# Gate and up as seven block products in place of eight, on equal token halves

## The chip, the core and the metric

The kernel runs on one core of a Trainium2 chip. Its engines work beside each other, each in its own fixed order of instructions, and wait for one another through semaphores: PE multiplies matrices (a matmul here is a 128x128 block of weights times up to 512 columns of activations) and writes to PSUM; DVE and POOL do elementwise work; ACT does elementwise work with a scale, a bias or a function; SP issues most transfers. The metric is the device time of one execution in microseconds, the median of several runs.

## The reference

Two transformer-like layers run over 128 prompt tokens and 512 sample tokens that share all weights. The model width is 1024, the width of the feed-forward part 2816. A layer has a mixer (short convolution, windowed attention and a gated delta rule, side by side), and then the part that this change is in:

```python
h2 = _rms(x, p['norm2_g']) * (1 + sc2) + sh2
x = x + g2 * ((jax.nn.silu(h2 @ p['w_gate']) * (h2 @ p['w_up'])) @ p['w_down'])
```

The vectors sc2, sh2 and g2 come from a conditioning vector of each token group (adaLN), so the prompt's 128 tokens have others than the sample's 512. Everything is float32.

## The kernel before

All activations of the feed-forward part are feature-major: a tile holds 128 features in its partitions and tokens in its columns, all 640 of them (the prompt first). The operands of a product are in the form fp32r, and each is split in a high part (a rounded copy, made by ACT) and a low part (the exact rest, made by DVE, or by POOL for some tiles of the norm). A product of two such operands takes three matmuls: high by high, low by high, high by low (`split` L173 and L174, `fm_product` L200 to L206). The tokens are taken in two parts, HB, of 256 and 384.

The feed-forward stage of a layer runs so:

- The mixer's output product (`rows` with w_out) adds to the residual `xt`, feature tile by feature tile (`residual`, L446); its last four feature tiles are one late group (LATE_OUT): first part 0 of all four, then the normalisation of part 0 (`Norm.half`), then part 1 and its normalisation. The normalisation squares, sums over the features on PE (L379, L381), takes the root on POOL (L386), spreads it over the partitions on PE (L389, into the bank `pkq`), and then makes per feature tile a scaled value t on DVE (L418), the high part on ACT (L423, L424, L427) and the low part on DVE or POOL (L425, L431).
- Gate and up: feature tiles f = 0 to 21 of 128 columns of w_gate and w_up. Per tile, 8 k tiles x 3 passes x 2 parts, 48 matmuls for gate and as many for up. Then tanh on ACT (L1524), silu on DVE (L1526), the product with up (L1533) and the split of the result. In the first two tiles (LEAD) the low parts of the activations come last, and part 0 of both tiles before part 1.
- Down: the 22 tiles are done in three chunks (FF_CHUNKS: 8, 8 and 6). After each chunk its rows of w_down are multiplied with it, one output feature tile at a time, and added to xt. In the last chunk of layer 0 the last three output tiles (LATE_DOWN) form a late group, with the next layer's norm behind each part; in layer 1 each finished tile is transposed, copied (L1560) and stored.
- Weights come as 512 KB transfers on SP's queue, three raw buffers deep; ACT and DVE split each (`load_w`, 128x1024 a tile). Between them stand steps of the next layer's adaLN product (`drain(gen, 1)`).

The order on each engine is set by a scheduler that follows the program order with priorities; what stands in it is seen below.

Of the kernel before, what the change touches and what calls it, by code (L numbers as in the profile page):

```python
# [23 lines left out]
KT_ = 8  # L24
TOK = 640
NT = 5
HB = ((0, 256), (256, 640))      # the two parts of the tokens that one product takes
HN = (256, 384)
# [12 lines left out]
FF_CHUNKS = ((0, 8), (8, 8), (16, 6))  # L41
WK_BUFS, CV_BUFS = 4, 4
RAW_BUFS, W_BUFS, SIDE_BUFS = 3, 2, 2
SG_BUFS, LEAD = 4, 2
# [8 lines left out]
LATE_DOWN = (5, 6, 7)  # L53

# column layout of the packed constants
# [8 lines left out]
def shape_constants():  # L64
    """Constants that depend on the shapes alone, packed as [128, C_TOTAL] float32."""
# [33 lines left out]
    near = 16 * (p // 64)              # first row of the near half of a 32-block: the half solved first  # L99
# [9 lines left out]
def hybrid_trunk_kernel(  # L109
# [15 lines left out]
    def atiles(pool, tag, name):  # L125
        """(hi, lo) of both token parts of one feature tile."""
        return tuple(tuple(pool.tile([128, HN[h]], F32R, tag=f"{tag}{h}", name=f"{name}{h}{x}", bufs=16) for x in "hl")
                     for h in range(2))

    def spans(a0, a1):  # L130
        """tokens a0..a1 cut at the parts' border: (part, columns of the part, tokens from a0)."""
        return [(h, slice(max(a0, b0) - b0, min(a1, b1) - b0), slice(max(a0, b0) - a0, min(a1, b1) - a0))
                for h, (b0, b1) in enumerate(HB) if max(a0, b0) < min(a1, b1)]

# [20 lines left out]
    # ---------------------------------------------------------------- constants  # L155
# [72 lines left out]
    # ---------------------------------------------------------------- small per-layer vectors  # L228
    # silu of the conditioning vectors: columns (sample, prompt) per k-tile, padded to 32
# [63 lines left out]
    def ada_pair(l, f, araw):  # L293
        """half f of the columns of the 1024-column pieces 0 and 1; a generator as ada."""
# [41 lines left out]
    class Norm:  # L336
# [10 lines left out]
        def ft(self, n, name):  # L347
            return self.fp.tile([128, n], F32, tag="ft", name=name, bufs=6)
# [1248 lines left out]
```

## Time and profile before

| | |
|---|---|
| median of 3 runs | 1807.85 us (1805.13 to 1810.63) |
| span of the profiled execution | 1806.5 us |
| median less that span | 1.35 us |
| PE busy in the span | 1725.5 us (96%) |
| DVE busy | 981.2 us (54%) |
| ACT busy | 636.2 us (35%) |
| POOL busy | 113.2 us (6%) |

The span is the time from the first to the last instruction of one execution that was recorded by the hardware profiler. The runs are timed without it, and what lies around a span isn't in the page; the difference above stands for it. The page's busy time of PE counts a matmul from its start to the modelled end, and neighbouring matmuls overlap, so a matmul's worth is the distance between two starts, not its duration. "Idle before" in a row is the time in which that engine waited just before the row's instructions, with the instruction that ended it.

### The profile page before, as it was taken

The numbers are of one execution on the slowest core, as the hardware profiler recorded it, in microseconds if no ns is written. First come the engines' busy times: TensorE is split into PE (matmuls) and PEld (weight loads), VectorE is DVE, ScalarE is ACT, GpSimd is POOL, SyncE is SP. The second block draws the span as 40 slices with busy tenths as digits, with TensorE's granted clock in tenths as the row PEclk, the third lists the DMA queues.
The fourth block names the chain that finished last, engine by engine and source line by source line (L and its number), as shares of the span: only waits on it lengthen the run. The fifth ranks groups of instructions, "written<-read, shape, count | busy, mean of one in ns | idle before, by whom it ended". The sixth has DMA issues, their size and how long they took to land. (4 is left out here: it accounts for less than half of the span.)

```text
span 1806.5 us, 34244 instructions
## 1 busy us (share of the span) xinstructions
PE 1725.5 (96%) x14179; PEld 1566.9 (87%) x14179; DVE 981.2 (54%) x2324; ACT 636.2 (35%) x1330; POOL 113.2 (6%) x230
## 2 busy tenths in 40 slices
PE   5998999999999999999999879999999999999998
PEld 3887875488999999999988879655899999999998
DVE  3799767666433333333477995777563333333333
ACT  3545244544322122212255442556352212221221
POOL 1111112000000000000012011220010000000000
PEclk7999999999999999999999989999999999999999
DMA  8512234656242222222232222455722222222222
GB/s 287 174 48 68 80 105 126 204 165 227 70 134 78 82 71 80 73 72 78 91 106 72 60 60 77 144 150 161 231 59 71 71 82 70 82 71 73 80 66 75
DMA packets 230025, 188.41 MB, mean 104 GB/s; under 512 B 11566, under 2 KB 206062, under 8 KB 229870
## 3 DMA queue, kind: packets, MB, share of 16 engines
q1 hardware_dynamic: 212992, 170.70, 31.4%
q10 hardware_dynamic: 16878, 15.53, 2.7%
q8 instruction: 111, 1.82, 0.4%
q14 instruction: 44, 0.36, 0.1%
HBM read 168.64 MB, written 17.56 MB: 103 GB/s over the span
## 5 line engine op out<-in xcount | busy, mean ns | idle before, releaser
L173 ACT CAST whi<-raw 128x1024 fp32r<-128x1024 f32 (+2 forms) x191 | 190.2, 996 | 598.9 <-PE pmm L202 271.5
L174 DVE TENSOR_TENSOR wlo<-raw,whi 128x1024 fp32r<-128x1024 f32 (+2 forms) x191 | 220.9, 1158 | 224.3 <-ACT whi L173 223.1
L200 PE MATMUL pmm<-hhi,whi 128*128 128x256 f32 x1008 | 319.0, 317 | 6.6 <-ACT dnp L517 5.3
L203 PE MATMUL pmm<-hhi,wlo 128*128 128x256 f32 x1008 | 317.4, 316 | 7.1 <-DVE wlo L174 7.1
L202 PE MATMUL pmm<-hlo,whi 128*128 128x256 f32 x960 | 301.7, 314 | 0.0
L200 PE MATMUL pmx<-hhi,whi 128*128 128x384 f32 (+1 forms) x688 | 213.0, 310 | 1.0 <-ACT hhi L427 0.7
L203 PE MATMUL pmx<-hhi,wlo 128*128 128x384 f32 (+1 forms) x688 | 212.9, 310 | 0.0
L200 PEld LDWEIGHTS pmm<-hhi,whi 128*128 128x128 f32 x1008 | 195.9, 194 | 11.1 <-ACT dnp L517 6.1
L203 PEld LDWEIGHTS pmm<-hhi,wlo 128*128 128x128 f32 x1008 | 195.7, 194 | 8.4 <-DVE wlo L174 7.7
L202 PE MATMUL pmx<-hlo,whi 128*128 128x256 f32 (+1 forms) x640 | 197.6, 309 | 0.0
L202 PEld LDWEIGHTS pmm<-hlo,whi 128*128 128x128 f32 x960 | 185.7, 193 | 0.7 <-issue 0.4
L200 PEld LDWEIGHTS pmx<-hhi,whi 128*128 128x128 f32 x688 | 130.3, 189 | 2.5 <-ACT hhi L427 1.5
L203 PEld LDWEIGHTS pmx<-hhi,wlo 128*128 128x128 f32 x688 | 130.3, 189 | 0.4 <-issue 0.4
L202 PEld LDWEIGHTS pmx<-hlo,whi 128*128 128x128 f32 x640 | 121.3, 190 | 0.0
L1533 DVE SCALAR_TENSOR_TENSOR av<-sg,pmx 128x256 f32<-128x256 f32 (+1 forms) x88 | 42.9, 488 | 131.8 <-PE pmx L203 123.9
L446 DVE SCALAR_TENSOR_TENSOR xt<-pmx,mod,xt 128x128 f32<-128x128 f32 (+1 forms) x96 | 39.1, 436 | 96.2 <-PE pmx L203 96.0
L446 DVE SCALAR_TENSOR_TENSOR xt<-pmm,mod,xt 128x128 f32<-128x128 f32 (+1 forms) x96 | 39.0, 436 | 91.6 <-PE pmm L203 89.1
L492 PE MATMUL pmm<-wlo,hhi 128*128 128x256 f32 x240 | 69.2, 289 | 0.7 <-DVE wlo L174 0.7
L491 PE MATMUL pmm<-whi,hhi 128*128 128x256 f32 x240 | 69.7, 292 | 0.0
L493 PE MATMUL pmm<-whi,hlo 128*128 128x256 f32 x240 | 69.3, 289 | 0.0
L1524 ACT ACTIVATE th<-pmm 128x256 f32<-128x256 f32 (+1 forms) x88 | 38.2, 434 | 76.7 <-PE pmm L203 70.7
L1526 DVE SCALAR_TENSOR_TENSOR sg<-th,pmm 128x256 f32<-128x256 f32 (+1 forms) x88 | 42.6, 485 | 41.1 <-ACT th L1524 41.1
(450 smaller groups left out, 3798.0 us busy)
## 6 DMA issues: line engine op xcount, KB each, us to landing
adaw<-in_ada_w_dram SPq DMA_DIRECT2D x64, 512.0 KB, 3.9
raw<-in_w_gate_dram SPq DMA_DIRECT2D x44, 512.0 KB, 3.9
raw<-in_w_up_dram SPq DMA_DIRECT2D x44, 512.0 KB, 3.9
raw<-in_w_in_dram SPq DMA_DIRECT2D x36, 512.0 KB, 4.8
araw<-in_ada_w_dram SPq DMA_DIRECT2D x32, 512.0 KB, 5.0
raw<-in_w_down_dram SPq DMA_DIRECT2D x32, 512.0 KB, 4.1
raw<-in_w_down_dram SPq DMA_DIRECT2D x16, 384.0 KB, 3.6
xm<-xscr SPq DMA_DIRECT2D x16, 320.0 KB, 4.9
```

The costliest lines, as they stand in the source:

```text
L173: (hi_eng or A.copy)(hi, src)
L174: (lo_eng or V).tensor_tensor(out=lo, in0=src, in1=hi.bitcast(F32), op=ALU.subtract)
L200: mm(o, lhsT=wh[:, k], rhs=ah, start=k == 0, stop=False)
L202: mm(o, lhsT=wh[:, k], rhs=al, start=False, stop=False)
L203: mm(o, lhsT=wl[:, k], rhs=ah, start=False, stop=not lead and k == n - 1)
L446: V.scalar_tensor_tensor(out=x[:, sl], in0=pt[:, a0:a1], scalar=gate[:, g:g + 1], in1=x[:, sl], op0=ALU.mult, op1=ALU.add)
L491: mm(pt, lhsT=ah[:, ts], rhs=wh[:, k % 4], start=k == 0, stop=False)
L492: mm(pt, lhsT=ah[:, ts], rhs=wl[:, k % 4], start=False, stop=False)
L493: mm(pt, lhsT=al[:, ts], rhs=wh[:, k % 4], start=False, stop=k == 7)
L1524: A.activation(th, pg[:, 0:n], AF.Tanh, scale=0.5)
L1526: V.scalar_tensor_tensor(out=sgs[h], in0=th, scalar=1.0, in1=pg[:, 0:n], op0=ALU.add, op1=ALU.mult)
L1533: V.scalar_tensor_tensor(out=av, in0=sgs[h], scalar=0.5, in1=pu[:, 0:n], op0=ALU.mult, op1=ALU.mult)
```

## The change

Two feature tiles of gate (or of up) are computed together as a 2 x 2 block product: the weights in blocks of 2 halves of k (four k tiles each) by 2 feature tiles, the activations in blocks of 2 halves of k by 2 halves of the tokens. Eight block products become seven, in the form of Strassen and Winograd: some operands are sums of blocks, and some results are sums of products. Token parts are now 320 and 320. The core of the diff:

```diff
-HB = ((0, 256), (256, 640))
+HB = ((0, 320), (320, 640))
-FF_CHUNKS = ((0, 8), (8, 8), (16, 6))
+FF_CHUNKS = ((0, 4), (4, 4), (8, 4), (12, 4), (16, 4), (20, 2))
-LATE_DOWN = (5, 6, 7)
+LATE_DOWN = tuple(range(8))
...
+    class PairNorm(Norm):
...
+        def half(self, h):
...
+            for j in range(4):
+                h12, h22 = self.ft(HH, "h12"), self.ft(HH, "h22")
+                self.value(j, 1, h12)
+                self.value(j + 4, 1, h22)
+                h11, h21 = self.first[j][:, 0], self.first[j][:, 1]
+                t3, t1, t2, t4 = (self.ft(HH, name) for name in ("nt3", "tt1", "tt2", "nt4"))
+                G.tensor_tensor(out=t3, in0=h12, in1=h22, op=ALU.subtract)
+                G.tensor_tensor(out=t1, in0=h12, in1=h11, op=ALU.subtract)
+                G.tensor_tensor(out=t2, in0=h22, in1=t1, op=ALU.subtract)
+                G.tensor_tensor(out=t4, in0=h21, in1=t2, op=ALU.subtract)
+                for name, src in (("nt3", t3), ("t1", t1), ("t2", t2), ("nt4", t4)):
+                    self.block(j, name, src, self.fp if n < 12 else apool)
...
+            held = pkq()
+            Y, Z = held[:, 0, 0:HH], held[:, 1, 0:HH]
+            for bank in (Y, Z):
+                mm(bank, lhsT=identr, rhs=B[0]["b11"][0], start=True, stop=True)
...
+                    with tc.high_priority():
+                        split(flat(D), flat(self.d[0]), flat(self.d[1]))
+                        V.tensor_tensor(out=flat(Pa), in0=flat(D), in1=flat(O)[:, 1:2].to_broadcast([128, 2, 512]), op=ALU.add)
+                        split(flat(Pa), flat(self.a[0]), flat(self.a[1]))
+                        split(O[:, 0], *self.o)
+                        V.tensor_tensor(out=Pb[:, 0], in0=Pa[:, 1], in1=D[:, 0], op=ALU.add)
+                        V.tensor_tensor(out=Pb[:, 1], in0=Pb[:, 0], in1=O[:, 0], op=ALU.add)
+                        split(flat(Pb), flat(self.b[0]), flat(self.b[1]))
+                def product(self, bank, w, name, start):
+                    wh, wl = w
+                    for j in range(4):
+                        bh, bl = B[j][name]
+                        mm(bank, lhsT=wh[:, j], rhs=bh, start=start and j == 0, stop=False, skip_group_check=True)
+                        mm(bank, lhsT=wh[:, j], rhs=bl, start=False, stop=False, skip_group_check=True)
+                        mm(bank, lhsT=wl[:, j], rhs=bh, start=False, stop=j == 3, skip_group_check=True)
...
+                def s4(self, hold=False):
+                    if hold:
+                        A.copy(Y, self.kept)
+                    self.product(Y, self.of(self.b, 0), "t2", False)
+                    A.copy(Z, Y)
+                    self.u = tp("u")
+                    A.copy(self.u, Y)
...
+                if ci == 0:
+                    p, q = Pair(*pairs[0]), Pair(*pairs[1])
+                    for step in (p.s1, p.s3, lambda: q.s1(True), q.s3, p.s2, p.s4, p.s5, p.s6, q.s2, p.s7, lambda: q.s4(True),
+                                 q.s5, q.s6):
+                        step()
...
+                for ms in (LATE_DOWN,) if last_chunk and norm else tuple((m, m + 1) for m in range(0, KT_, 2)):
+                    drain(gen, None if last_chunk else 1)
+                    rows(ms, w_down[l], f0, nf, act, mods[l][:, 40:48], norm if last_chunk else None, True,
+                         nf - 2 if ms == (0, 1) else None)
```

Each `product` is 12 matmuls of 320 columns (L1645 to L1647), and a pair of feature tiles has seven: s1 with the block b11 of the first token half, s3 with b21, and s2, s4, s5, s6, s7 with nt3, t2, nt4, t1 and nb22, all from the second half or from both. D holds two weight blocks, O the other two, and Pa and Pb are their sums (L1634, L1637, L1638, DVE); D, Pa, Pb and one block of O are split. Y and Z are two accumulators in one bank that is held for the whole stage and is the same kind of tile as the one that holds the norm's spread root. s1 copies its result, negated, to Y; s2 copies its own to w7; s4 copies Y to Z and to u; s5 and s6 add u and w7 on DVE (c21, c22). The down product takes its first two output tiles with the chunk's last two feature tiles last (`lead` = nf − 2). Residual adds are now of 128, 192 and 320 columns (L528).

On PE, where layer 0's feed-forward stage starts, before: the sums (L381) and the spread (L389) of part 1 stand among first-part products; hhi and hlo are the norm's high and low parts, whi and wlo those of the weights.

```order
1882 L381 MATMUL pxo<-ones_c,sq 128x1 x3
1883 L206 MATMUL pmx<-hlo,whi 128x256 x4
1884 L389 MATMUL pkq<-ident,ny 128x128 x3
1885 L206 MATMUL pmx<-hlo,whi 128x256
1886 L203 MATMUL pmm<-hhi,wlo 128x256
1887 L200 MATMUL pmm<-hhi,whi 128x256
...
1901 L206 MATMUL pmm<-hlo,whi 128x256 x8
1902 L200 MATMUL pmx<-hhi,xhi 128x256
```

Now, at the same place: b_ are blocks of the first half, nt_ are nt3 of j = 0 to 3, ohi is the high part of O.

```order
1869 L406 MATMUL pkq<-ident,ny 128x80 x4
1870 L1645 MATMUL pmm<-b_5606,whi 128x320
...
1874 L1645 MATMUL pmx<-nt_5747,xhi 128x320
...
1878 L1645 MATMUL pmx<-nt_5778,xhi 128x320
...
1881 L1645 MATMUL pmx<-nt_5809,xhi 128x320
...
1884 L1606 MATMUL pkq<-b_5579,identr 128x320 x2
1885 L1645 MATMUL pmm<-b_5614,ohi 128x320
...
1897 L1645 MATMUL pmx<-nt_5840,xhi 128x320
```

Behind the spread came a long row of products with first-part activations (1885 to 1901 and on); now three matmuls with b_ remain there (1870 to 1872), and the products with nt3 of three j's stand ahead of the two that fill the held bank (L1606) and of p.s3 (ohi).

On ACT, the second token part of that stage, before: each tile's high part is one ACTIVATE or an ACTIVATE and a CAST.

```order
439 L427 ACTIVATE hhi<-t_5759,mod_97 128x384
440 L423 ACTIVATE t_5766<-t_5764,mod_97 128x384
441 L173 CAST act0h<-av 128x256
442 L424 CAST hhi<-t_5766 128x384
443 L427 ACTIVATE hhi<-t_5772,mod_97 128x384
444 L1524 ACTIVATE th<-pmm 128x256
445 L423 ACTIVATE t_5780<-t_5778,mod_97 128x384
446 L424 CAST hhi<-t_5780 128x384
```

And now: L482 is a value of the second half, L469 the high part of a block, L513 that of nb22.

```order
467 L482 ACTIVATE h_5731<-t_5733,mod_97 128x320
468 L482 ACTIVATE h_5732<-t_5736,mod_97 128x320
469 L469 CAST nt_5747<-nt_5739 128x320
470 L469 CAST t_5750<-tt_5740 128x320
471 L469 CAST t_5753<-tt_5741 128x320
472 L469 CAST nt_5756<-nt_5742 128x320
473 L513 ACTIVATE nb_5759<-h_5732 128x320
474 L482 ACTIVATE h_5762<-t_5764,mod_97 128x320
475 L482 ACTIVATE h_5763<-t_5767,mod_97 128x320
476 L469 CAST nt_5778<-nt_5770 128x320
```

Two values, four high parts and nb22 of one j now stand ahead of the next j's values (474, 475).

On POOL at the same place, before: L386 is the root, L425 a low part of the norm.

```order
84 L386 TENSOR_TENSOR ny<-nms,mhalf 128x3
85 L425 TENSOR_TENSOR hlo<-t_5766,hhi 128x384
86 L425 TENSOR_TENSOR hlo<-t_5780,hhi 128x384
87 L425 TENSOR_TENSOR hlo<-t_5794,hhi 128x384
```

Now: four operations per j on values that ACT makes (h_), 16 in the stage.

```order
82 L503 TENSOR_TENSOR nt_5739<-h_5731,h_5732 128x320
83 L504 TENSOR_TENSOR tt_5740<-h_5731,h_5573 128x320
84 L505 TENSOR_TENSOR tt_5741<-h_5732,tt_5740 128x320
85 L506 TENSOR_TENSOR nt_5742<-h_5573,tt_5741 128x320
86 L503 TENSOR_TENSOR nt_5770<-h_5762,h_5763 128x320
```

POOL's low parts went to DVE, and the sums nt3, tt1, tt2 and nt4 came in their place.

## Rows read from the trace of the kernel before

**Rows 1.** Windows: the two FFN stretches and the layer-1 start; busy (count) per engine.
```profile
core 0: us, PE busy (x) PEld busy (x) DVE busy (x) ACT busy (x) POOL busy (x), PEclk, DMA share, GB/s
441.00:936.00 495.00, 492.62 (x3404) 485.06 (x3397) 195.72 (x345) 126.26 (x212) 8.51 (x10) 0.99 0.30 89
1337.00:1802.00 465.00, 462.29 (x3139) 460.51 (x3139) 173.17 (x284) 109.59 (x168) 3.05 (x3) 1.00 0.25 72
1322.70:1337.00 14.30, 13.43 (x101) 12.83 (x100) 9.37 (x25) 6.66 (x17) 1.63 (x2) 0.92 0.22 65
```

**Rows 2.** Timeline of PE: start, duration; steps of 384, 256, 272 columns.
```profile
527.85 0.34 PE L200 MATMUL pmm<-hhi,whi 128*128 128x384 f32 x1
...
532.02 0.28 PE L200 MATMUL pmx<-hhi,whi 128*128 128x256 f32 x1
...
534.89 0.34 PE L200 MATMUL pmx<-hhi,whi 128*128 128x384 f32 x1
...
947.79 0.29 PE L491 MATMUL pmm<-zw,hhi 128*128 128x272 f32 x1
...
951.06 0.29 PE L493 MATMUL pmm<-zw,hlo 128*128 128x272 f32 x1
```

**Rows 3.** Groups by form, DVE: line, names, shapes, count | busy us, mean ns | idle.
```profile
L174 DVE TENSOR_TENSOR wlo<-raw,whi 128x1024 fp32r<-128x1024 f32 x160 | 195.6, 1224 | 213.2 <-ACT whi L173 213.0
...
L174 DVE TENSOR_TENSOR act1l<-av,act1h 128x384 fp32r<-128x384 f32 x44 | 24.3, 552 | 1.2 <-ACT act1h L173 1.2
...
L174 DVE TENSOR_TENSOR act0l<-av,act0h 128x256 fp32r<-128x256 f32 x44 | 19.2, 437 | 19.9 <-ACT act0h L173 19.9
...
L174 DVE TENSOR_TENSOR wlo<-raw,whi 128x512 fp32r<-128x512 f32 x16 | 11.0, 686 | 1.9 <-ACT whi L173 1.7
```

**Rows 4.** Groups by form, ACT, same columns.
```profile
L173 ACT CAST whi<-raw 128x1024 fp32r<-128x1024 f32 x160 | 167.8, 1049 | 528.5 <-PE pmm L202 250.9 <-PE pmx L202 225.1 <-issue 22.5
...
L173 ACT CAST act1h<-av 128x384 fp32r<-128x384 f32 x44 | 22.4, 509 | 6.6 <-DVE av L1533 6.6
...
L173 ACT CAST act0h<-av 128x256 fp32r<-128x256 f32 x44 | 17.9, 406 | 85.9 <-DVE av L1533 85.9
...
L427 ACT ACTIVATE hhi<-t,mod 128x384 fp32r<-128x384 f32 x20 | 12.0, 614 | 16.5 <-DVE t L418 16.5
```

**Rows 5.** Groups by form, POOL: low parts of the norm, same columns.
```profile
L425 POOL TENSOR_TENSOR hlo<-t,hhi 128x384 fp32r<-128x384 f32 x12 | 12.5, 1044 | 22.9 <-ACT hhi L424 22.4 <-PE pmx L206 0.6
...
L425 POOL TENSOR_TENSOR hlo<-t,hhi 128x256 fp32r<-128x256 f32 x12 | 10.5, 874 | 54.2 <-ACT hhi L424 54.2
```

**Rows 6.** Timeline of DVE, layer-1 FFN start: start, duration, what, [idle before <-releaser].
```profile
1311.84 0.61 DVE L446 SCALAR_TENSOR_TENSOR xt<-pmx,mod,xt 128x128 f32<-128x128 f32 x2 [0.80 <-PE pmx L203]
...
1316.76 2.16 DVE L418 SCALAR_TENSOR_TENSOR t<-xt,msc,pkq 128x128 f32<-128x128 f32 x8 [0.21 <-PE pkq L389]
...
1320.75 1.57 DVE L431 SCALAR_TENSOR_TENSOR hlo<-t,mod,hhi 128x128 fp32r<-128x128 f32 x2
...
1322.51 0.60 DVE L431 SCALAR_TENSOR_TENSOR hlo<-t,mod,hhi 128x128 fp32r<-128x128 f32 x2
...
1329.22 0.61 DVE L446 SCALAR_TENSOR_TENSOR xt<-pmx,mod,xt 128x384 f32<-128x384 f32 x1
...
1336.09 2.19 DVE L418 SCALAR_TENSOR_TENSOR t<-xt,msc,pkq 128x384 f32<-128x384 f32 x4 [0.77 <-PE pkq L389]
```

**Rows 7.** Timeline of POOL and ACT in the same stretch.
```profile
1319.95 2.22 POOL L425 TENSOR_TENSOR hlo<-t,hhi 128x256 fp32r<-128x256 f32 x2 [3.99 <-ACT hhi L424]
...
1339.30 1.02 POOL L425 TENSOR_TENSOR hlo<-t,hhi 128x384 fp32r<-128x384 f32 x1 [4.80 <-ACT hhi L424]
...
1338.71 0.52 ACT L424 CAST hhi<-t 128x384 fp32r<-128x384 f32 x1
```

**Rows 8.** Windows at the border of the layers, columns as in rows 1.
```profile
905.00:916.00 11.00, 10.54 (x83) 10.22 (x81) 5.47 (x15) 2.83 (x5) 0.69 (x1) 1.00 0.58 172
916.00:950.00 34.00, 32.15 (x200) 30.06 (x201) 26.48 (x54) 22.77 (x49) 6.75 (x14) 0.95 0.34 97
```

**Rows 9.** Timeline of PE, last transposes of the kernel.
```profile
1801.63 0.55 PE L1556 MATMUL pmx<-ident,xt 128*128 128x128 f32 x3 [0.60 <-DVE xt L446]
```

More of the change, by code (lines that the diff above doesn't have):

```diff
@@ L206, in fm_product, with fm_part @@
                 mm(o, lhsT=wh[:, k], rhs=acts[k][h][1], start=False, stop=k == n - 1)
+    def fm_part(pt, wh, wl, acts, h, ks, first, last):
+        o = pt[:, 0:HH]
+        for k in ks:
+            ah, al = acts[k][h]
+            mm(o, lhsT=wh[:, k], rhs=ah, start=first and k == ks[0], stop=False)
+            mm(o, lhsT=wh[:, k], rhs=al, start=False, stop=False)
+            mm(o, lhsT=wl[:, k], rhs=ah, start=False, stop=last and k == ks[-1])
     def rsqrt_dve(src, n, scale, eps, posts, name):
@@ L344, in __init__ @@
             self.bc = [None, None]
-            self.out = [[None, None] for _ in range(KT_)]
+            self.out = [None] * KT_
         def ft(self, n, name):
-            return self.fp.tile([128, n], F32, tag="ft", name=name, bufs=6)
+            return self.fp.tile([128, n], F32, tag=self.tag, name=name, bufs=self.bufs)
         def add(self, k, parts=(0, 1)):
@@ L410, in high @@
             b0, b1 = HB[h]
[L411 removed]
+            n = HH
             sh, bc_ = self.sh, self.bc[h]
[L413 to L414 removed]
+            if self.out[k] is None:
+                self.out[k] = Act(apool, "a", "h")
+            hi, lo = self.out[k][h]
             x = self.xt[k][:, b0:b1]
@@ L433, in high, with __init__, ft, block @@
             return low
+    class PairNorm(Norm):
+        def __init__(self, fp, xt, a_fn, sh, late):
+            super().__init__(fp, xt, a_fn, sh, late)
+            self.out = [{} for _ in range(4)]
+            self.first = [None] * 4
+        def ft(self, n, name):
+            return self.fp.tile([128, n], F32, tag="tp", name=name, bufs=TP_BUFS)
+        def block(self, j, name, src, pool):
+            if pool is apool:
+                b = pool.tile([128, 2, HH], F32R, tag="a", name=name, bufs=16)
+            else:
+                b = pool.tile([128, 2, HH], F32R, tag="bx", name=name, bufs=12)
+            A.copy(b[:, 0], src)
+            V.tensor_tensor(out=b[:, 1], in0=src, in1=b[:, 0].bitcast(F32), op=ALU.subtract)
+            self.out[j][name] = (b[:, 0], b[:, 1])
+        def value(self, k, h, dst):
+            b0, b1 = HB[h]
+            segs = ((1, slice(0, 128)), (0, slice(128, HH))) if h == 0 else ((0, slice(0, HH)),)
+            t1 = self.ft(HH, "t1")
+            for g, sl in segs:
+                V.scalar_tensor_tensor(out=t1[:, sl], in0=self.xt[k][:, b0:b1][:, sl], scalar=self.a_[0][:, k, g:g + 1],
+                                       in1=self.bc[h][:, sl], op0=ALU.mult, op1=ALU.mult)
+            for g, sl in segs:
+                A.activation(dst[:, sl], t1[:, sl], AF.Identity, bias=self.sh[:, k, g:g + 1])
+        def half(self, h):
+            if 0 not in self.a_:
+                self.a_[0] = self.a_fn(0, KT_)
+            self.stats(h)
+            if h == 0:
+                for i in range(2):
+                    for j in range(4):
+                        if i == 0:
+                            self.first[j] = self.fp.tile([128, 2, HH], F32, tag="act", name="h0", bufs=8)
+                        self.value(j + 4 * i, 0, self.first[j][:, i])
+                        self.block(j, ("b11", "b21")[i], self.first[j][:, i], apool)
+                return
+            n = 0
+            for j in range(4):
[10 more added lines that the diff above has]
+                    self.block(j, name, src, self.fp if n < 12 else apool)
+                    n += 1
+                pool = self.fp if n < 12 else apool
+                n += 1
+                b = pool.tile([128, 2, HH], F32R, tag="a" if pool is apool else "bx", name="nb22", bufs=16 if pool is apool else 12)
+                A.activation(b[:, 0], h22, AF.Copy, scale=-1.0)
+                V.scalar_tensor_tensor(out=b[:, 1], in0=h22, scalar=-1.0, in1=b[:, 0].bitcast(F32), op0=ALU.mult, op1=ALU.subtract)
+                self.out[j]["nb22"] = (b[:, 0], b[:, 1])
```

251 lines of the change are left out of this document (149 added, 102 removed).

## The prediction

> **What bounds the kernel now.** I read the page's busy shares first (PE 96% of the span, DVE 54%, ACT 35%, POOL 6%), then a table of windows, then groups by form, and last the order of time at the start of a feed-forward stage. The two stretches of gate, up and down products, one per layer, hold PE busy 492.62 of 495 us and 462.29 of 465 us at granted clock 0.99 and 1.00, while DVE works 40% of them and ACT 25% [rows 1]. PE is idle 5 us in 960. So a matmul left out there is worth its full spacing, as long as the new work beside PE really stays beside it. That has two places: the steady pairs, where DVE has room, and the start of each feed-forward stage, where the activations are prepared and PE has little else to do.
>
> **What a matmul is worth.** Mean durations of PE rows overlap, so I take starts: 24 matmuls of 384 columns take 532.02 − 527.85 = 4.17 us, 173.8 ns each; 24 of 256 take 2.87 us, 119.6 ns each [rows 2]. A straight line through both gives 146.7 ns at 320 and 126.4 at 272; the trace has 26 steps of 272 in 3.27 us, 125.8 ns [rows 2]. I use 146.4 ns. A pair of feature tiles had 96 matmuls of 320 columns on average and now has 84. There are 44 pairs (11 gate and 11 up in each of two layers), so 44 × 12 × 0.1464 = **−77.3 us**. The down product keeps its columns: 0. Equal halves alone: 0.
>
> **Durations at 320 columns**, between the rows of 256 and 384: a DVE low part or sum 0.49 us (0.437, 0.552) [rows 3]; an ACT cast or copy 0.46 (0.406, 0.509), an ACT scale with bias 0.56 (under 0.614 at 384) [rows 4]; a POOL tensor_tensor 0.96 (0.874, 1.044) [rows 5]; a DVE scaled value t from its spacing, 2.16 us for eight of 128 and 2.19 for four of 384, so 0.27 and 0.55, hence 0.34 at 192 and 0.48 at 320 [rows 6].
>
> **The start of the feed-forward stage.** Before, first-half products need only the high and low parts of the normed activations, and the second part's preparation runs behind them. Now five operand blocks per j (nt3, t1, t2, nt4, nb22) come from both token halves, for j = 0 to 3. In the order of PE the third step of the list, p.s3, stands behind products of nt3 of j = 0, 1 and 2 and behind the two matmuls that fill the held bank, and that bank is the one out of which the last j's values are read. So PE waits for nearly the whole preparation. I count from the start of the last residual add of the first half (in the layer-1 stage 1311.84 [rows 6]).
> First values: +4.9, as before (1316.76). DVE's list up to the last second-half residual: 8 × (0.27 + 0.34) = 4.9 of values, 8 × 0.49 = 3.9 of low parts, two weight low parts 2 × 1.22 and two half sums 2 × 0.69 [rows 3], four residual adds, put at 0.55 as a low part of 384 [rows 3], one square sum 0.49: 15.3. That ends at +20.2. From there to the first second-half value passed 1336.09 − 1329.83 = 6.3 us before [rows 6] (squares, their sums on PE, the root, the spread), and the same steps stand now: +26.5. Two values, two biases and hops: first h22 at +28.2.
> Then one cycle per j, serial as ACT and DVE have it in their order: the next j's values stand on DVE behind this j's nb22 low part, that behind ACT's nb22, that behind ACT's cast of nt4, and that waits for the fourth POOL operation. 4 × 0.96 + 0.46 + 0.46 + 0.49 + 2 × 0.48 + 0.56 + five hops of 0.07 (an ACT cast that ends at 1339.23 lets POOL start at 1339.30 [rows 7]) = 7.1 us. Three cycles bring the last h22 to +49.5; POOL 3.84, then on ACT nt4, nb22, the cast of O (512 columns, between 0.51 and 1.05 [rows 4], 0.62), tanh and hops, before q.s3 can start: about +55.5 to 56.
> PE's work until then: 48 second-half output products (7.0 us), 58 matmuls of the new order (8.5) and sums, spreads and adaLN steps (near 3): 18.5. Idle 37.3, of which 0.9 was there before (13.43 busy of 14.30 in 1322.7 to 1337 [rows 1]): +36.4 a layer. If DVE and ACT overlap neighbouring instructions better than the means, 30; with collisions of DVE and POOL, 44.
> On these: two low parts took 1.57 us beside two POOL operations and 0.60 with POOL idle [rows 6, 7], and the new list sets three low parts per j beside POOL. I let 0.15 us a cycle of it onto the path and take 37 a layer, **+74 us** (60 to 88).
> [...]
>
> **Steady pairs.** PE now needs 84 × 0.1464 = 12.3 us a pair. DVE: four weight operations of 1024 columns (4 × 1.22: low parts of D, Pa, Pb and the sum Pa), three of 512 (3 × 0.69) [rows 3], 7.0 us; and in a gate pair six of 320 columns (four sg, c21, c22; 2.9), in an up pair ten (4.9): 9.9 and 11.9, mean 10.9, 88% of PE's time. Before, DVE had 40% of these stretches. ACT has some 7.4 us. So the weight work hides, but the short waits between copies (Y, Z, u, w7) and the products that follow them do not always: 0 to 0.4 us a pair, I take 0.2 × 40 = **+8** (0 to 16). Ramp after the start, with weight buffers late: **+3** (0 to 6). Six down chunks in place of three: products of the first four tiles of a group cover the last up product's chain (0.49 + 0.46 + 0.49), but in each layer's last chunk, of two tiles, nothing leads: 2 × 1.5 = **+3** (0 to 6).
>
> **Between the layers.** Before, PE is idle 0.46 + 1.85 us in 905 to 950 [rows 8]: three tiles stand in the late group, and their second part's products (54 matmuls of 384, 9.4 us) cover the first part's normalisation. Now all eight stand in it, with two k each: 48 matmuls, 7.0 us, and four of their residual adds stand on DVE behind the normalisation of the first half, a list of 15 us. At least the cover lost, 2.4 us, at most the list uncovered, 14: **+8**.
> **The end.** After the last product came one tile's transposes, copy and store; PE waited 0.60 us for the residual there [rows 9]. Now two tiles come at once and eight tiles leave inside 14 us of PE: **+4** (0 to 8).
> **The clock.** The granted clock is 0.92 in 1322.7 to 1337 [rows 1], where PE waits 0.9 us, so the stage's start has a dip now. The long wait will have one too; what runs slowly inside the wait costs nothing, and what comes behind it may. 0 ± 3.
>
> **Sum:** −77.3 + 74 + 8 + 3 + 3 + 8 + 4 = +22.7. The profiled span is 1806.5 us, 1.35 under the median of the runs (1807.85); I add the same 1.35: 1806.5 + 22.7 + 1.35 = **1830.5 us**.
>
> **Rivals.**
> *B, the preparation is mostly hidden.* If POOL runs its 16 operations nearly back to back (three cycles of 3.84 in place of 7.1) and the first half's list is shorter by its overlaps, idle falls to 20 a layer; with 12 for all the rest −77.3 + 40 + 12 = −25: 1782.5, faster. For it: back-to-back DVE values take 0.27, not their mean. Against: the fixed order of ACT and DVE, which puts j + 1 behind j. It decides below 25 us a layer.
> *C, DVE becomes the bound of gate and up.* Its 88% is an average; an up pair has 11.9 of 12.3. Waits on ACT and collisions of 1.4 us a pair close the mean gap; at 2.4 PE waits a full 1.0 us a pair: 40 × 1.0 in place of 8, 1862, slower.
> *D, the change doesn't gain what it says:* a matmul of 320 columns spaced as one of 384 (173.8 ns): 27 ns × some 6000 matmuls, over 1950. The 272 rows speak against it.
>
> **Chances.** Forecast 0.62 (own range 1808 to 1852), B 0.18, C 0.17, D 0.03. A measurement here tells about 0.3% (5.4 us) from no change. Faster: B's 0.18 less its part near zero, 0.03, plus 0.02 of the forecast's low tail, 0.17; same: that 0.03 and 0.05 of the forecast, 0.08; slower 0.75. The range 1794 to 1862 leaves out most of B (0.12) and D with half of C's tail (0.08).
>
> **What would show it.** Right: after the first b11 products PE idles some 37 us a layer, its waits naming the casts and low parts of nt3, t1 and O; 16 POOL rows of about 0.96 us per layer, every four of them 7 us after the last four; PE's spacing 146 ns at 320 columns; pairs 12.3 to 12.7 us apart. Wrong: a j cycle near 4 us (B), pairs over 13 us with PE waiting on low parts of weights (C), PE idle under 5 us between the layers.

## The result and the profile after

The changed kernel takes 1881.63 us (median of 4 runs, 1875.28 to 1885.66) against 1806.62 for the kernel before on the same chip: a ratio of 1.0401, 95% interval 1.0371 to 1.0431, 75 us slower. 1830.5 was forecast, in a range of 1794 to 1862. The sign was right, the size three times too small.

The page's busy line of the kernel after (it was 96%, 54%, 35% and 6%):

```profile
PE 1710.1 (91%) x13741; PEld 1519.0 (81%) x13741; DVE 1262.7 (67%) x2796; ACT 799.2 (43%) x1644; POOL 131.0 (7%) x250
```

Windows of the kernel after: the two stretches of gate, up and down, and four of 10 us at the start of layer 0's; columns as in [rows 1] (PEld is PE's loading of weights).

```profile
448.70:941.00 492.30, 455.20 (x3004) 429.79 (x3004) 309.47 (x516) 192.26 (x331) 15.66 (x17) 0.96 0.29 85
1373.60:1862.00 488.40, 447.63 (x2899) 431.02 (x2898) 310.62 (x519) 192.53 (x331) 15.65 (x17) 0.95 0.22 65
450.00:460.00 10.00, 3.49 (x16) 1.35 (x15) 7.70 (x17) 5.78 (x17) 0.00 (x0) 0.80 0.52 157
460.00:470.00 10.00, 9.67 (x52) 8.91 (x51) 0.92 (x3) 0.18 (x1) 1.01 (x1) 0.50 0.00 0
470.00:480.00 10.00, 4.46 (x20) 1.60 (x19) 5.13 (x10) 4.98 (x11) 5.78 (x7) 0.50 0.33 105
480.00:490.00 10.00, 2.32 (x5) 1.17 (x5) 7.08 (x12) 4.51 (x10) 5.20 (x6) 0.50 0.00 0
```

PE is idle 37 and 41 us in the two stretches, where it was 2 or 3 [rows 1], and at the start the granted clock is 0.50 for some 30 us. DVE's busy share went from 40% to 63%.

PE in the same stretch of the kernel after, timeline:

```profile
458.62 1.06 PE L286 MATMUL pdn<-adaw,c 128*32 128x256 f32 x2 [6.51 <-DMA adaw<-in_ada_w_dram]
...
479.20 0.64 PE L1645 MATMUL pmx<-nt,xhi 128*128 128x320 f32 x1 [3.12 <-ACT nt L469]
...
486.02 0.64 PE L1645 MATMUL pmx<-nt,xhi 128*128 128x320 f32 x1 [5.24 <-ACT nt L469]
...
490.92 0.87 PE L1606 MATMUL pkq<-b,identr 128*128 128x320 f32 x2 [3.32 <-DVE t L479]
...
502.01 0.31 PE L1645 MATMUL pkq<-t,xhi 128*128 128x320 f32 x1
...
503.62 0.31 PE L1647 MATMUL pkq<-t,xlo 128*128 128x320 f32 x1
...
966.84 0.61 PE L199 MATMUL pmm<-hh,whi 128*128 128x320 f32 x1 [8.09 <-DVE xt L528]
```

Rows 502.01 and 503.62 are 11 steps of 320 columns in 1.61 us, 146.4 ns: the gain per matmul is the one forecast from [rows 2]. Ahead of them PE waits for the cast of nt3 once per j, and for the last value t before it may fill the held bank, as forecast. The row at 966.84 is the border of the layers: 8.09 us for a residual add.

POOL and then DVE beside it, timelines (DVE's rows: last residual add of the first half and of the second, [rows 6] for before; the mean squares; the first second-half values; a low part beside POOL and one after it):

```profile
477.80 0.86 POOL L503 TENSOR_TENSOR nt<-h,h 128x320 f32<-128x320 f32 x1 [3.07 <-ACT h L482]
...
480.62 0.99 POOL L506 TENSOR_TENSOR nt<-h,tt 128x320 f32<-128x320 f32 x1
...
484.62 0.86 POOL L503 TENSOR_TENSOR nt<-h,h 128x320 f32<-128x320 f32 x1 [3.01 <-ACT h L482]
```

```profile
435.92 0.68 DVE L528 SCALAR_TENSOR_TENSOR xt<-pmx,mod,xt 128x128 f32<-128x128 f32 x2 [0.73 <-PE pmx L202]
...
457.20 0.55 DVE L528 SCALAR_TENSOR_TENSOR xt<-pmx,mod,xt 128x320 f32<-128x320 f32 x1
...
465.91 0.16 DVE L401 TENSOR_SCALAR nms<-pxo 80x4 f32<-80x4 f32 x1 [8.17 <-PE pxo L398]
...
469.24 1.01 DVE L479 SCALAR_TENSOR_TENSOR t<-xt,msc,pkq 128x320 f32<-128x320 f32 x2 [3.17 <-PE pkq L406]
...
480.00 0.90 DVE L470 TENSOR_TENSOR t<-tt,t 128x320 fp32r<-128x320 f32 x1 [0.17 <-ACT t L469]
...
482.14 0.49 DVE L470 TENSOR_TENSOR nt<-nt,nt 128x320 fp32r<-128x320 f32 x1 [0.17 <-ACT nt L469]
```

A j cycle is 484.62 − 477.80 = 6.82 us (7.1 forecast), a sum on POOL 0.86 to 0.99 (0.96 forecast). A low part takes 0.49 us alone and 0.90 beside POOL; [rows 6, 7] had that in two rows.

A border between two chunks of layer 1, DVE and then PE: the new pairs' weight work (pa, pb and their low parts xlo) and a low part of the down product's own weights (wlo<-raw) stand between the parts of residual adds, and PE waits for these.

```profile
1556.43 0.34 DVE L528 SCALAR_TENSOR_TENSOR xt<-pmm,mod,xt 128x128 f32<-128x128 f32 x1
1556.69 1.22 DVE L173 TENSOR_TENSOR xlo<-pa,xhi 128x1024 fp32r<-128x1024 f32 x1
1557.83 0.68 DVE L1638 TENSOR_TENSOR pb<-pb,rawo 128x512 f32<-128x512 f32 x1
1558.43 0.41 DVE L528 SCALAR_TENSOR_TENSOR xt<-pmm,mod,xt 128x192 f32<-128x192 f32 x1
...
1559.02 1.22 DVE L173 TENSOR_TENSOR wlo<-raw,whi 128x1024 fp32r<-128x1024 f32 x1
1560.15 1.22 DVE L173 TENSOR_TENSOR xlo<-pb,xhi 128x1024 fp32r<-128x1024 f32 x1
1561.29 0.41 DVE L528 SCALAR_TENSOR_TENSOR xt<-pmx,mod,xt 128x192 f32<-128x192 f32 x1
```

```profile
1558.99 0.39 PE L199 MATMUL pmm<-acth,whi 128*128 128x320 f32 x1 [1.15 <-DVE xt L528]
...
1561.84 0.39 PE L199 MATMUL pmx<-acth,whi 128*128 128x320 f32 x1 [0.85 <-DVE xt L528]
```

To place the time, the trace is cut at the first and last matmul of each output product and at the last of each down product. Spans between the cuts, worked out from the starts of those rows in each trace (us; the kernels e1 to e11 are those of the next section):

| kernel | mixer 0 | output 0 | FFN 0 | mixer 1 | output 1 | FFN 1 |
|---|---|---|---|---|---|---|
| before | 362.2 | 77.6 | 484.0 | 322.0 | 76.6 | 478.1 |
| after | 365.2 | 83.3 | 509.9 | 330.8 | 84.3 | 499.7 |
| e9 old parts | 360.5 | 78.4 | 487.6 | 327.1 | 77.6 | 482.4 |
| e7 halves | 364.5 | 80.8 | 490.3 | 330.7 | 78.0 | 482.6 |
| e1 eight products | 367.1 | 82.2 | 489.9 | 331.4 | 78.2 | 483.3 |
| e4 residual first | 362.9 | 80.4 | 497.7 | 329.1 | 80.9 | 485.8 |
| e8 no weight sums | 363.7 | 82.1 | 483.3 | 330.6 | 84.1 | 471.4 |
| e11 bare | 365.1 | 82.5 | 459.4 | 331.7 | 82.6 | 449.8 |

One trace of each; the first mixer alone differs by up to 10 us between kernels that share its code (360.5 to 371.0), so single columns are read only for large differences. The execution traced for e4 took 1844.94 us, 11 less than the median of its runs, so its row flatters it.

### The profile page after: what moved, and what is told of

Its sections match the earlier page's. It is cut to its first block, busy times and chain, and to the rows that moved or that the text cites. A ratio compares the mean times of both kernels' runs of the same rounds, so it can differ in the third digit from the quotient of the medians.

```text
span 1879.7 us, 34411 instructions
## 1 busy us (share of the span) xinstructions
PE 1710.1 (91%) x13741; PEld 1519.0 (81%) x13741; DVE 1262.7 (67%) x2796; ACT 799.2 (43%) x1644; POOL 131.0 (7%) x250
## 4 chain that ended last, share of the span: by engine, by line
PE 42%; issue 30%; DVE 13%; DMA 9%; ACT 4%; POOL 2%; SPq 0%; ACTq 0%; DVEq 0%; POOLq 0%
PE pmm L202 3%; PE pmm L199 3%; PE pmm L201 3%; DVE wlo L173 2%; DMA adaw<-in_ada_w_dram 2%; PE pdn L286 2%; PE pmm L1339 2%; PE pmx L1377 2%; PE pmx L199 2%; PE pkq L1645 1%; PE pmx L202 1%; PE pmx L1372 1%; PE pmx L201 1%; PE pkq L1646 1%; DMA rawo<-in_w_up_dram 1%
## 5 line engine op out<-in xcount | busy, mean ns | idle before, releaser
L172 ACT CAST whi<-raw 128x1024 fp32r<-128x1024 f32 (+2 forms) x108 | 101.2, 937 | 176.3 <-PE pmx L201 50.9
L173 DVE TENSOR_TENSOR wlo<-raw,whi 128x1024 fp32r<-128x1024 f32 (+2 forms) x108 | 116.8, 1083 | 30.6 <-ACT whi L172 30.4
L199 PE MATMUL pmm<-hh,whi 128*128 128x320 f32 x336 | 111.7, 332 | 12.6 <-DVE xt L528 8.1
L202 PE MATMUL pmm<-hh,wlo 128*128 128x320 f32 x336 | 111.5, 332 | 7.6 <-DVE wlo L173 7.6
L1645 PE MATMUL pkq<-t,xhi 128*128 128x320 f32 x352 | 109.5, 311 | 0.6 <-DVE sg L1705 0.6
L1646 PE MATMUL pkq<-t,xhi 128*128 128x320 f32 x352 | 109.0, 310 | 0.0
L1647 PE MATMUL pkq<-t,xlo 128*128 128x320 f32 x352 | 109.0, 310 | 0.0
L201 PE MATMUL pmm<-hl,whi 128*128 128x320 f32 x320 | 103.6, 324 | 0.0
L199 PE MATMUL pmm<-acth,whi 128*128 128x320 f32 x272 | 86.2, 317 | 13.2 <-DVE xt L528 12.7
L528 DVE SCALAR_TENSOR_TENSOR xt<-pmx,mod,xt 128x128 f32<-128x128 f32 (+2 forms) x168 | 69.7, 434 | 35.8 <-PE pmx L202 34.9
L199 PE MATMUL pmx<-acth,whi 128*128 128x320 f32 x272 | 85.3, 313 | 5.2 <-DVE xt L528 5.2
L528 DVE SCALAR_TENSOR_TENSOR xt<-pmm,mod,xt 128x128 f32<-128x128 f32 (+2 forms) x168 | 70.0, 434 | 25.0 <-PE pmm L202 22.4
L201 PE MATMUL pmm<-actl,whi 128*128 128x320 f32 x272 | 85.5, 314 | 0.0
L1645 PE MATMUL pmx<-nt,xhi 128*128 128x320 f32 x176 | 58.6, 333 | 27.1 <-ACT nt L469 22.1
```

The costliest lines, as they stand in the source:

```text
L199: mm(o, lhsT=wh[:, k], rhs=ah, start=k == 0, stop=False)
L201: mm(o, lhsT=wh[:, k], rhs=al, start=False, stop=False)
L202: mm(o, lhsT=wl[:, k], rhs=ah, start=False, stop=not lead and k == n - 1)
L528: V.scalar_tensor_tensor(out=x[:, sl], in0=pt[:, a0:a1], scalar=gate[:, g:g + 1], in1=x[:, sl], op0=ALU.mult, op1=ALU.add)
L1645: mm(bank, lhsT=wh[:, j], rhs=bh, start=start and j == 0, stop=False, skip_group_check=True)
L1646: mm(bank, lhsT=wh[:, j], rhs=bl, start=False, stop=False, skip_group_check=True)
```

## The experiments

All ratios are to the kernel before, run beside each kernel on the same chip, with a 95% interval; times are medians of four runs (e9: six).

**e1: eight products.** The block products are undone, the rest of the change stays.

```diff
-            norm = PairNorm(fp, xt, ...)
+            norm = Norm(fp, xt, ...)
...
-                    pairs += [(w_gate[l], f0 + fi, gate), (w_up[l], f0 + fi, up)]
+                for i in range(nlead, nf):
+                    gw, uw, sgs = ffn_load(f0 + i)
+                    gate_half(gw, sgs, 0), gate_half(gw, sgs, 1), up_half(uw, sgs, act[i], 0), up_half(uw, sgs, act[i], 1)
```

> The changed kernel with the eight products of before in gate and up (96 matmuls a pair of feature tiles), without operand sums, weight sums and the held bank; the equal token halves, the six chunks and the late group of all eight output tiles stay. Theory 1 (the block products bring the loss: preparation at the start of the stage, about 31 us a layer beyond before, bursts of weight work on DVE that hold up residual adds in the output product and at chunk borders, about 13 and 25 us): 77 us of matmuls come back and about 120 us of waits go, 1825 to 1840 us; what stays over before is the border of the layers (10 to 14 us) and some us at chunk borders. Rival (halves, chunks and late group bring the loss): over 1860 us.

1841.23 us, 1.0178 (1.0155 to 1.0201). About the size expected from theory 1 (its upper end was 1840), but what it left over was not where I put it (e7): the block products cost 2.2 points net, and 1.8 points stay without them.

**e2: without the second half's preparation.**

```diff
...
-                for name, src in (("nt3", t3), ("t1", t1), ("t2", t2), ("nt4", t4)):
-                    self.block(j, name, src, self.fp if n < 12 else apool)
...
+                for name, of in (("nt3", "b21"), ("t1", "b11"), ("t2", "b21"), ("nt4", "b11"), ("nb22", "b21")):
+                    self.out[j][name] = self.out[j][of]
```

> The changed kernel without the second half's normalisation and sums in the feed-forward norm: the first half's blocks b11 and b21 stand in for nt3, t1, t2, nt4 and nb22, so the output is another. Seven products, weight work and chunks stay. Theory 1 (the start's wait is set by that preparation, 36 and 35 us lost in the two stages, some 6 of them in before too): 1815 to 1825 us, 55 to 65 less than the changed kernel. Rival (other work, DVE's weight sums, would hold PE at that place anyway): less than 30 us gained, over 1850 us.

1837.58 us, 1.0135 (1.0097 to 1.0173): 2.7 points, some 48 us, less than the 55 to 65 expected and far more than the rival's 30. The first 84 matmuls of the block products, 53.3 and 50.2 us long in the two layers of the kernel after, take 31.8 and 28.2.

**e3: all values of the second half first, then the sums.**

```diff
+            for j in range(4):
+                ...
+                self.value(j, 1, h12)
+                self.value(j + 4, 1, h22)
+                hv.append((h12, h22))
             for j in range(4):
-                self.value(j, 1, h12)
-                self.value(j + 4, 1, h22)
+                h12, h22 = hv[j]
```

> The changed kernel with the loop over j of the second half cut in two: all eight values of the second half first, then the sums of j = 0 to 3, so that POOL's 16 operations stand back to back. Theory 1 (the 6.8 us per j are a serial chain POOL, ACT, DVE, ACT, of which POOL needs 3.7): three cycles shorten by 3.1 us each, 9 us a layer, 1860 to 1868 us. Rival (the wait is set by PE's sums and spread at half clock and by the first half's list, not by the cycle): within 5 us of the changed kernel's 1881.

1877.45 us, 1.0386 (1.0354 to 1.0418): nothing that can be told from the kernel after. POOL's sums now stand back to back, as meant, and the time went into DVE's low parts. DVE and then POOL in layer 1 of e3:

```profile
1405.32 1.14 DVE L470 TENSOR_TENSOR nt<-nt,nt 128x320 fp32r<-128x320 f32 x1
...
1406.39 2.22 DVE L470 TENSOR_TENSOR t<-tt,t 128x320 fp32r<-128x320 f32 x2
...
1416.00 0.48 DVE L470 TENSOR_TENSOR nt<-nt,nt 128x320 fp32r<-128x320 f32 x1
```

```profile
1398.96 0.86 POOL L507 TENSOR_TENSOR nt<-h,h 128x320 f32<-128x320 f32 x1 [5.22 <-ACT h L482]
...
1405.13 0.99 POOL L509 TENSOR_TENSOR tt<-h,tt 128x320 f32<-128x320 f32 x1
...
1407.15 1.11 POOL L507 TENSOR_TENSOR nt<-h,h 128x320 f32<-128x320 f32 x1
```

Beside POOL each low part takes 1.1 us, one per POOL operation, and the same operation 0.48 once POOL is done (1416.00). The time is the rival's, but not for the rival's reason: the first 84 block products take 50.2 and 48.4 us, and 45.6 and 44.0 in e5, which keeps this order and takes the sums off POOL (50.3 and 50.4 in e4, which does neither). My theory had the chain right for the kernel as it stood and missed the collision that replaces it.

**e4: residual adds ahead of the weight work on DVE.**

```diff
-                        residual(xt[m], pt, h, gate[:, m])
+                        with tc.high_priority():
+                            residual(xt[m], pt, h, gate[:, m])
```

> The changed kernel with the residual adds of the output and down products given priority over the weight work on DVE. Theory 1 (PE's waits for PSUM banks, 24 us in the trace put down to residual adds, come from bursts of weight work ahead of them): PE's waits for residual adds fall under 8 us and the time to 1862 to 1870 us. Rival (the weight work that is pushed back is as urgent, and the first products of the next pairs wait for it): 1878 to 1890 us, the waits then named by low parts of weights.

1855.98 us, 1.0248 (1.0215 to 1.0281): 1.5 points, 27 us, more than expected. PE's waits for residual adds (us in total, times, longest), after and then e4:

```profile
PE pmm L199 <- DVE xt L528: 24.3, 12, 8.1
PE pmx L199 <- DVE xt L528: 7.1, 8, 1.0
```

```profile
PE pmm L199 <- DVE xt L528: 2.4, 6, 0.8
```

The rival is refuted: the weight work that was pushed back did not hold up the next pairs. The longest wait, 8.1 us, is the one at the border of the layers, which stands in e1 too, without the block products (e12).

**e5: e4, values first, sums on DVE.**

```diff
-                G.tensor_tensor(out=t3, in0=h12, in1=h22, op=ALU.subtract)
+                V.tensor_tensor(out=t3, in0=h12, in1=h22, op=ALU.subtract)
```

(and the same for t1, t2 and t4.)

> e4 (residual adds first) with the values of the second half first, as in e3, and the 16 sums of each stage on DVE in place of POOL. Theory (while POOL runs a sum, DVE gets one low part through per POOL operation: in e3 each took 1.1 us beside POOL and 0.48 after it, so POOL's sums and DVE's low parts share one chain): without POOL the 36 operations of the list take 0.41 us each and the last operand is there 27.5 - 18.5 = 9 us after the first value sooner; PE can use some 5 to 8 us of it in each layer: 10 to 16 us under e4, ratio to before 1.016 to 1.019. Rival (no collision; DVE, with 16 operations more, is the longer chain): e4's ratio 1.025 or above.

1841.03 us, 1.0173 (1.0148 to 1.0198): 0.75 points under e4, as expected. Order and engine changed together; the order alone brought nothing that could be told (e3). A low part of the list now takes 0.48 us, so 16 more operations on DVE are cheaper than POOL's help. DVE in e5:

```profile
473.43 0.48 DVE L507 TENSOR_TENSOR nt<-h,h 128x320 f32<-128x320 f32 x1
...
474.75 0.48 DVE L470 TENSOR_TENSOR nt<-nt,nt 128x320 fp32r<-128x320 f32 x1
```

**e6: e4 with the late group in two.**

```diff
-                for ms in (LATE_DOWN,) if last_chunk and norm else ...
+                for ms in (LATE_DOWN[0:4], LATE_DOWN[4:8]) if last_chunk and norm else ...
```

> e4 with the down product of the last chunk of layer 0 in two groups of four output tiles in place of one of eight, so that the next layer's norm stands behind four tiles. Theory (four residual adds of the second half stand on DVE behind the norm of the first half, and PE waited 8.1 us for one there in the changed kernel): PE's wait for a residual add at the border goes, 5 to 9 us under e4, mixer stage of layer 1 from 329 to 321 to 324 us. Rival (e4 has removed that wait already; what is left is the norm itself): within 3 us of e4.

1849.29 us, 1.0211 (1.0174 to 1.0248). The intervals of e4 and e6 overlap; FFN 0 is 3.7 us shorter in the trace and mixer 1 is 8.9 longer (338.0; but it is 337.1 in e2 and e12 too, without this edit). In e4's trace no wait for a residual add of more than 0.8 us is left, so what the edit was to remove had gone already, as the rival says. Inconclusive in time.

**e7: equal halves alone.** e1 with the chunks and late group of before.

```diff
-FF_CHUNKS = ((0, 4), (4, 4), (8, 4), (12, 4), (16, 4), (20, 2))
+FF_CHUNKS = ((0, 8), (8, 8), (16, 6))
-LATE_DOWN = tuple(range(8))
+LATE_DOWN = (5, 6, 7)
```

> e1 (eight products on equal halves) with the chunks and the late group of before (8, 8 and 6 tiles, down tiles 5 to 7 late): of the change only the equal halves are left, with the sums of squares in pieces of 80 columns. Theory (equal halves cost little by themselves; e1's 32 us over before come from the late group of eight and the six chunks): 1812 to 1822 us, ratio 1.003 to 1.008. Rival (the halves cost it: the first part's preparation is longer for 320 columns and the second part has less to cover it): 1835 us or more, ratio over 1.014.

1835.54 us, 1.0160 (1.0119 to 1.0200). My theory falls, the rival holds: nearly all that e1 left over is here, and six chunks with the late group add nothing that can be told (1.0178 against 1.0160). That it is the halves themselves takes e9.

**e8: e4 without weight sums.**

```diff
-                    self.a, self.b = ([fp.tile([128, 2, 4, 128], F32R, tag=tag, name=tag, bufs=SIDE_BUFS) for tag in ("xhi", "xlo")]
-                                      for _ in range(2))
+                    self.a = self.b = self.d
...
```

> e4 without the weight sums: Pa and Pb are neither formed nor split, D's parts stand in for them (the output is another); DVE loses 5.1 us of work a pair (three operations of 1024 and two of 512 columns), ACT 2.1. Theory (what is left of the loss between the starts, some 20 us a layer, and of the longer output product is DVE's weight work): 18 to 30 us under e4, ratio to before 1.008 to 1.015. Rival (the losses are hops, copy to product, product to sum): under 8 us.

1823.92 us, 1.0082 (1.0055 to 1.0110): 1.7 points under e4, at the upper end of the expectation. The two feed-forward stages are 14.4 us shorter each; the output products are not (82.1 and 84.1 us, 80.4 and 80.9 in e4), so that part of the theory falls. The edit takes work from DVE and from ACT together and doesn't tell them apart. Two waits of the kernel after are gone from e8's list and stay in e4's, the first for ACT's high parts of the weight sums; PE's waits in the kernel after, columns as in e4:

```profile
PE pmx L1645 <- ACT xhi L172: 5.0, 8, 1.1
PE pmx L1647 <- DVE xlo L173: 1.6, 3, 0.9
```

**e9: e7 with the token parts of before.**

```diff
-HB = ((0, 320), (320, 640))
+HB = ((0, 256), (256, 640))
```

> e7 (eight products, chunks and late group of before) with the token parts of before, 256 and 384, and sums of squares in pieces of 128: only the side edits of the change are left (one tile for both parts, raw weights of adaLN in the common ring, ten temporary tiles of 384). Theory (e7's 1.6% over before comes from the equal halves: the first part's preparation is 25% longer and the second part's products cover it less): 1806 to 1816 us, ratio 0.999 to 1.004. Rival (side edits and another order of the scheduler cost it): ratio 1.010 or above.

1819.08 us, 1.0060 (1.0035 to 1.0085), between the two expectations: the halves account for 1.0 point (about ± 0.5, from the two intervals) and the side edits, with another order of the scheduler, for 0.6.

**e10: e5 with PE kept busy.**

```diff
+                        for _ in range(fill):
+                            mm(idle, lhsT=identr, rhs=B[0]["b11"][0], start=True, stop=True)
```

> e5 with 72 more matmuls of 320 columns on a spare bank at each start of the feed-forward stage (nothing reads them), so that PE has something to do where it waited. Theory (part of the start's loss is PE at granted clock 0.5 to 0.67 for some 40 us behind the first wait, with the sums of squares and then the first products on the path): the granted clock stays above 0.9 there, the matmuls behind it take 147 ns, 6 to 10 us a layer come back: 12 to 20 us under e5, ratio to before 1.006 to 1.011. Rival (operands, not PE, set the path there, so a faster PE only waits longer, and the added matmuls stand in the way): ratio 1.016 to 1.022.

1838.28 us, 1.0165 (1.0141 to 1.0190): e5's time. The clock did rise where the added matmuls stood; window of e5 and then of e10, columns as above:

```profile
450.00:460.00 10.00, 7.33 (x46) 5.62 (x47) 2.60 (x7) 3.61 (x11) 1.01 (x1) 0.52 0.36 113
```

```profile
450.00:460.00 10.00, 10.00 (x86) 10.00 (x85) 5.99 (x16) 6.64 (x19) 0.00 (x0) 1.00 0.39 106
460.00:470.00 10.00, 8.70 (x43) 7.43 (x43) 5.56 (x13) 5.02 (x12) 1.01 (x1) 0.66 0.07 11
480.00:490.00 10.00, 8.11 (x32) 6.58 (x31) 5.29 (x13) 4.36 (x11) 0.00 (x0) 0.59 0.02 6
```

but not behind them throughout (0.66 in 460 to 470, 0.59 in 480 to 490), and FFN 0 and 1 are only 3.5 and 2.3 us shorter. The time is the rival's: what clock came back moved the time by nothing that can be told. A start at full clock throughout was not reached, so what that would be worth stays open.

**e11: seven products without what prepares them** (e2, e4 and e8 together).

> The changed kernel with residual adds first (e4), without weight sums (e8) and without the second half's normalisation and sums (e2): seven products on halves, without the work that prepares them (the output is another). Theory (the losses add up): 1.0401 - 0.0153 (e4) - 0.0166 (e8) - 0.0266 (e2) = 0.982 of before, 1770 to 1785 us, which is the 77 us of matmuls less the halves and side edits (1.6%) and some border work. Rival (the three overlap, or the matmuls left out don't bring 77 us): 0.990 of before or above, over 1790 us.

1774.02 us, 0.9831 (0.9806 to 0.9857), as the theory worked out (0.982). PE in that kernel's layer 0:

```profile
440.00:930.00 490.00, 482.28 (x3238) 461.90 (x3238) 234.96 (x465) 159.29 (x313) 6.72 (x8) 0.97 0.30 92
```

PE is idle 8 us in 490. The three losses add up. Against e1, which has eight products on the same halves, the two feed-forward stages are 64 us shorter, where the matmuls left out are 77; behind the start (from the 85th block product to the last) e11's matmuls still take some 10 us a layer more than 146.4 ns each.

**e12: e1 with the residual adds first.**

> e1 (eight products on equal halves, six chunks) with the residual adds first, as in e4. Theory (the queue of residual adds comes from the block products' weight work on DVE, which e1 doesn't have): gain under a third of e4's 1.5%, only at the border of the layers, ratio to before 1.012 to 1.019. Rival (halves and chunks hold up the residual adds by themselves): ratio 1.002 to 1.008.

1832.92 us, 1.0146 (1.0119 to 1.0174): 0.3 points under e1, not told apart from it, against 1.5 in e4. So the queue of residual adds at chunk borders and in the output products is the block products' own. The wait at the border of the layers is not: e1 has it without them, and it is the only wait for a residual add of more than 0.2 us in e1's trace; in e12 it is gone. e1 there:

```profile
949.05 0.61 PE L199 MATMUL pmm<-hh,whi 128*128 128x320 f32 x1 [9.58 <-DVE xt L528]
```

## Why the prediction was wrong

The step that failed is the price of the work behind the start of each stage: steady pairs, ramp and chunk borders, put at 14 us for both layers because DVE's work fits into PE's time on average. It lost 61 us. Beside it two terms put at nothing were not nothing: the output products lost 13 us, and equal halves alone cost about 1.0 point (18 us), spread over these places. By place, in us, from the spans of the traces before and after:

| place | forecast | measured |
|---|---|---|
| 528 matmuls less, at 146.4 ns | −77 | −77 |
| starts of the two feed-forward stages | +74 | +64 |
| rest of these stages: pairs, ramp, chunk borders | +14 | +61 |
| output products | 0 | +13 |
| mixers, with the border of the layers | +8 | +12 |
| end | +4 | +0.5 |
| sum | +23 | +73 |

A start is the time of the first 84 block products above 146.4 ns each (41.0 and 37.9 us), less the same for the first products of as many columns before (8.2 and 6.6).

By cause, in points of the time before (1 point is 18 us), each from two ratios above; each ratio is uncertain by 0.25 to 0.4, so a difference by about 0.4:

| term | forecast | measured | from |
|---|---|---|---|
| 528 matmuls less | −4.3 | −4.3 | spacing 146.4 ns |
| start of the stage: second half's preparation | +4.1 | +2.7 | after, e2 |
| of it POOL and DVE in one another's way, and order | +0.1 | +0.75 | e4, e5 |
| steady pairs, ramp, chunk borders | +0.8 | +3.2 | 1.5 (after, e4) and 1.7 (e4, e8) |
| equal halves | 0 | +1.0 | e7, e9 |
| side edits | not priced | +0.6 | e9 |
| six chunks and late group, border and end | +0.7 | +0.2 | e1, e7 |

The measured rows give −4.3 + 2.7 + 3.2 + 1.0 + 0.6 + 0.2 = 3.4 of 4.0 points; 0.6 stay open, about what their uncertainties allow. What e4 and e8 take away lies in part at the starts (the first 84 block products take 48.7 and 45.5 us in e8) and in the output products, so the 3.2 are not all of the row's own place.

**Gain of the matmuls: right**, in size and place.

**Start of the stage: right mechanism and nearly the size, with errors that offset one another.** The order of waits, the POOL rows and the cycle were as forecast. The first second-half value stood later than forecast behind the first half's last residual add: 33.3 us (469.24 − 435.92) in layer 0 and 31.6 in layer 1, not 26.5. DVE's list up to there took 21.8 and 23.0 us and not 20.2, and the way from there to the value 11.5 and 8.6 and not 6.3: in layer 0 PE took until 465.91 for the sums of squares of values that DVE had finished at 457.75, at granted clock 0.50 and behind adaLN products that had waited 6.51 us for their weights. Against that, the wait is not all idle: the gaps between PE's rows add up to 21.5 and 22.5 us and not 37, and 19.5 and 15.4 us more went into PE's work in the same time, the block products above 146.4 ns (8.6 and 8.7) and the sums, spreads and adaLN products between them (10.9 and 6.7). I had priced such work at full clock and had said that what runs slowly inside the wait costs nothing. And the kernel before lost 8.2 and 6.6 us at the same place, where I subtracted the 0.9 of its idle time. Nor does the whole loss hang on the second half's preparation: without it (e2) 48 us come back, and e2's first 84 products still lose 21 us more than before.

**Steady pairs: the step that failed.** I compared DVE's work with PE's time as an average, 88%, and priced the rest as hops of 0.2 us. The work is not spread evenly: weight operations have priority and come in bursts, two pairs' worth at a chunk's border and in the output product, and the residual adds queue behind them. In layer 1 of the trace, counted from one pair's product with t1 to the next pair's, 15 steps inside chunks are 13.5 us on average and not 12.3 (12.3 to 12.7 was forecast), and the five that hold a border's down products, 40.4 us of matmuls, are 42.3. e4 takes the borders to 39.8 and leaves the steps inside at 13.4; e8 takes those to 12.4. From the 85th block product to the last, PE's matmuls in layer 1 take 31.5 us more than 146.4 ns each, 17.3 in e4 and 8.1 in e8, where I had 7 (layer 0, without its adaLN products: 28.3, 20.2 and 10.5). So about half of what I missed there was the order of a queue, and most of the rest the weight sums themselves. The output products, where I had priced nothing, are 5.7 and 7.7 us longer than before, 3.2 and 1.4 of it without block products too (e7); e4 gave back 2.9 and 3.4.

**"Equal halves alone: 0": wrong.** I counted columns. The halves cost 1.0 point without any block product. e7's trace shows PE idle 2.7 and 4.2 us more than before in the mixers and 2.9 and 2.5 in the FFNs, and the first part of each norm is now 320 tokens with 320 instead of 384 behind it to cover it. That it is this cover was argued, not shown; another order of the mixer's instructions may share in it. The same holds for the 0.6 points of the side edits.

**Border of the layers: the size in the trace is luck.** The wait that I described is there (8.09 us; 8 forecast), but mixer 1 is 8.8 us longer than before in the kernel after and 8.7 in e7, which has the late group of before and no such wait; the border's own worth could not be told from nothing (e1 against e7; e1 against e12; e6).

**The rivals.** B asked for under 25 us of idle a layer at the start, and the gaps are under 25; but its reason, a j cycle near 4 us, didn't come (6.82), and the gain didn't either, since the start's loss stood in slow PE work as well. C named DVE as the bound above 88%, and its sign, pairs over 13 us apart, did come; but DVE is 63% busy, and about half of what I missed in the pairs went away by order alone (e4). The truth was between A, the forecast, and C: a queue in the wrong order, and the weight work itself. D is refuted by the 146.4 ns.

No kernel that computes the reference with seven products came under the kernel before: the best are e10 and e5, at 1.0165 and 1.0173. Even without the weight sums e8 stays at 1.0082.

## What to carry to other kernels

A change that trades matmuls for elementwise work must be priced by the queue that the new work joins, not by that engine's average: ask what stands behind each burst and who waits for it, and put the small operations that free PSUM banks first (27 us in e4). Before pricing a new algorithm, price its preconditions by themselves (here equal token halves), since they cost even where they change no count (1.0 point, e7 and e9). And an idle engine isn't free help: with all values first, moving the sums from POOL to the busier DVE was faster (first 84 block products 45.6 and 44.0 us in e5, 50.2 and 48.4 in e3).

## What the runs showed of the hardware

A low part of 128x320 on DVE (L470) takes 0.48 us alone, 0.90 beside POOL's sums in the kernel after (480.00), and 1.1 us, one per POOL operation, where POOL's sums stand back to back (e3). POOL's own sum nt3 (L507) goes from 0.86 to 1.1 us there. The runs show these times, not what holds the two engines up. I had let 0.15 us a cycle of this onto the path; it took up what the reordering of e3 was to gain.

In the kernel after, PE's granted clock is 1.00 in 454 to 456 and 0.50 in 457 to 458, both inside its wait of 6.51 us that ends at 458.62, and it is still 0.50 in 460 to 470, where PE is busy 9.67 of 10 us. In e10, with the clock at 1.00 in 450 to 460 (0.52 in e5) and 0.66 in 460 to 470, the time moves by nothing that can be told (1.0165 against 1.0173).
